# First row block of the scores from a joint key matmul, and three smaller moves, in a one-core encoder block

## The chip, the cores and the metric

The kernel runs on one core of one Trainium2 chip. The metric is the device time of one execution in microseconds, as the median of several; lower is better. A profiled execution gives, beside its time, a record of every instruction on the engines: PE (matmuls) and PEld (the weight loads that go with them), DVE (vector), ACT (scalar), POOL (a slower vector engine) and SP (here a queue that issues transfers).

## The reference

One layer of an encoder block on a 512 x 2048 input in float32, with eight stick-breaking heads (`sb`), eight forgetting heads (`fox`) and a squared-ReLU layer of width 8192. What matters here are the scores of a head, q k^T, block of 128 rows by block, each row block i with (i+1)*128 key columns:

```python
for i in range(seq // Q_BLOCK):
    end = (i + 1) * Q_BLOCK
    qb = q[:, :, i * Q_BLOCK:end]
    kb = k[:, :, :end]
    z = jnp.einsum('bhqd,bhkd->bhqk', qb, kb).astype(jnp.float32) * scale
    ...
x = x + jnp.einsum('bse,ed->bsd', mixed, w_out[l])
```

The fox heads add a bias to z and take a softmax; the sb heads take log-sigmoids, a reversed running sum and an exponential. Both end in a product with v, a per-head norm, and a slice of `mixed`, which the output projection multiplies.

## The kernel before

All matrix products run in a rounded 32-bit format. To keep float32 accuracy each operand is split in a high part (ACT casts it) and a low part (DVE subtracts: source minus high), and each product is three matmuls, high x high, high x low, low x high. `mm3` (lines 76 to 79) issues them, which is why most matmuls of the profile stand on L77, L78 and L79.

The stages in order: first projections (to about 160 us), the heads (about 165 to 610 us), the output projection (to about 750 us), and the two large layers to the end. The heads run as a pipeline of 17 periods of about 26 us, the eight fox heads first. In period n PE projects q and k of head n (`accq`, 96 matmuls), computes the scores of head n-1 into the PSUM tile `s` (`Head.scores`, L792), the product with v of head n-2 (tile `o`), and the two matmuls that sum squares for that head's norm (tile `ssq`, `norm_sums`, L938 and L939). A head's work between scores and product: fox adds the bias on DVE (`start`, L840), takes row maxima (L847), exponentials on ACT (L852), a scaling on DVE (L857); sb does absolute value, exponential and logarithm on ACT (L806 to L810), DVE and POOL work, and a last exponential (L823). The result `w` is transposed by a transfer, or for the last head on PE (`turn`, L867), and split (`ph`, `pl`, L884 and L887). After the product, `square` (L928 to L930) and `square_low` (L933) make the operands of `ssq`.

The order of the work in this stage is written out by hand: `plan.at(time, function)` puts each step at a planned time, `Plan.run` sorts by it, and for PE, ACT and DVE the program keeps that order. Each engine works through its own list in order; an instruction that waits holds everything behind it. The planned times only sort. SP's order is made by the scheduler after the first periods.

Between the heads' work the same stage prepares sums of the output weights, in pairs of blocks. `whole(m, t)` does the first four of these: `load` (two transfers of 1 MB, L968), then for each of two sides a cast and a subtraction (`high` L972, `low` L975, tile `tboth`, which is then stored), and four differences (`sum`, L980). For m = 1 the first side was planned at 10.7 and 11.15 us, and the first difference at 16.3 us, into a period.

The projections' weights come in pieces (`wraw`, L163), split by ACT (L170, tile `wh`) and DVE (L177, tile `wl`).

After the heads, `g_form` (through `a_form` and `split`, L59 and L60) makes seven split left operands `g` from `mixed`, piece by piece; `out_piece` multiplies them with the output weights into `accoa`, `accob` and `accoc`.

Of the kernel before, what the change touches and what calls it, by code (L numbers as in the profile page):

```python
# [8 lines left out]
F32 = mybir.dt.float32  # L9
F32R = mybir.dt.float32r  # L10
U16 = mybir.dt.uint16
AF = mybir.ActivationFunctionType
ALU = mybir.AluOpType
PSUM = bass.MemoryType.PSUM

P = 128
NT = 512
# [3 lines left out]
NH = 8  # L21
# [11 lines left out]
OFF_Q = [256, 0, 384, 768]  # L33
# [4 lines left out]
def block_kernel(ctx, tc, x, g_attn, w_in, b_f, g_out_sb, g_out_fox, w_out, g_mlp, w_up, w_down, g_final, y):  # L38
# [59 lines left out]
    def u_tile(c):  # L98
        return tuple(up.tile([P, NT], F32R, tag=f"u{p}{c}", name=f"u{p}") for p in "hl")
# [119 lines left out]
    with ExitStack() as stage:  # L219
# [23 lines left out]
        plan = Plan()  # L243
# [469 lines left out]
    with tc.tile_pool(name="att", bufs=1, side="right", reuse_waits="tile") as at, \  # L713
# [25 lines left out]
                dve.scalar_tensor_tensor(f, ps, SCALE, rb, op0=ALU.mult, op1=ALU.mult)  # L739

        def high_u(i, which):
            u_of[i, which] = u_tile(i % 2 * 2 + which)
            act.copy(u_of[i, which][0], now["qf"])

        def low_u(i, which):
# [27 lines left out]
        def rows(w):  # L773
            return [w[:, OFF_Q[i]:OFF_Q[i] + (i + 1) * P] for i in range(TB)]
# [12 lines left out]
        class Head:  # L787
# [4 lines left out]
            def scores(self):  # L792
                q, k = u_of[self.i, 0], u_of[self.i, 1]
                s = atp.tile([P, 1536], F32, tag="s", name="s")
                for i in (3, 2, 0, 1):
                    n = (i + 1) * P
                    qs = slice(i * P, (i + 1) * P)
                    mm3(s[:, 2 * P + OFF_Q[i]:2 * P + OFF_Q[i] + n], q[0][:, qs], q[1][:, qs], k[0][:, :n], k[1][:, :n], i != 0, True)
                self.s = s[:, 2 * P:]

            def plan_sb(self, plan, t):
                g = self.h
# [27 lines left out]
            def plan_fox(self, plan, t):  # L830
                h = self.h - NH

                def load():
                    self.cb = at.tile([P, NT], F32, tag="ul5", name="cb")
                    sp.dma_start(self.cb, ckd[h:h + 1, :].to_broadcast([P, NT]))

                def start():
                    w = self.w = wide("w")
                    for i, r in enumerate(rows(self.s)):
                        dve.scalar_tensor_tensor(rows(w)[i], r, cq[:, i, h:h + 1], self.cb[:, :(i + 1) * P], op0=ALU.add, op1=ALU.add)  # L840
                    causal(w, ALU.is_ge, NEG)

                def maxed():
                    ml = at.tile([P, P], F32, tag="ml", name="ml")
                    self.mx, self.l = ml[:, :TB], ml[:, 16:16 + TB]
                    for i, r in enumerate(rows(self.w)):
                        dve.tensor_reduce(self.mx[:, i:i + 1], r, axis=mybir.AxisListType.X, op=ALU.max)  # L847
                    dve.tensor_scalar(self.mx, self.mx, -1.0, None, op0=ALU.mult)

                def soft():  # L850
                    for i, r in enumerate(rows(self.w)):
                        act.activation(r, r, AF.Exp, bias=self.mx[:, i:i + 1], accum_out=self.l[:, i:i + 1])  # L852

                def scale():
                    dve.reciprocal(self.l, self.l)
                    for i, r in enumerate(rows(self.w)):
                        dve.tensor_scalar(r, r, self.l[:, i:i + 1], None, op0=ALU.mult)  # L857

                for dt, f in zip((-4.0, 7.5, 12.4, 14.8, 17.5), (load, start, maxed, soft, scale)):
                    plan.at(t + dt, f)  # L860
# [134 lines left out]
        def whole(m, t):  # L995
            w = WeightSums(m, (0, 1), lambda: mixed[:, :NH].rearrange("p (q a) n -> p q (a n)", a=2))
            e, o = (t, t + TPER) if m else (TPER, TPER)
            loads = (0.5 if m == 1 else -15.0, 2.7) if m else (20.5, 20.6)
            highs, lows_, sums_, sixth = ((e + 3.3, o + 3.3), (e + 4.5, o + 4.5), (e + 6.4, e + 16.3, o + 6.4, o + 16.3), (o + 10.7, o + 20.6)) if m > 1 else \
                ((e + 10.7, o + 3.3), (e + 11.15, o + 4.5), (e + 16.3, e + 24.9, o + 6.4, o + 16.3), (o + 10.7, o + 20.6)) if m else \  # L1000
                ((e + 4.0, e + 10.0), (e + 5.2, e + 11.0), (e + 6.4, e + 19.2, e + 20.6, e + 21.8), (e + 22.0, e + 24.0))
            for i in range(2):
                plan.at(t + loads[i], w.load, (i,))
                plan.at(highs[i], w.high, i)
                plan.at(lows_[i], w.low, i)
            for i in range(4):
                plan.at(sums_[i], w.sum, i)
            plan.at(sums_[1] + 0.1, lambda: w.store(0, 2))
            plan.at(sixth[0], w.high_6)
            plan.at(sixth[1], w.low_6)  # L1010
            plan.at(sixth[1] + 0.1, lambda: w.store(2, 4))
# [44 lines left out]
        for n in range(2 * NH + 1):  # L1056
# [49 lines left out]
            if 0 <= i_s < 2 * NH:  # L1106
                H = heads[i_s]
                plan.at(t + (5.45 if n < 2 * NH else 4.4), H.scores)
                sb = H.h < NH
                (H.plan_sb if sb else H.plan_fox)(plan, t)  # L1110
                if n < 2 * NH:
                    plan.at(t + (24.7 if sb else 22.0), H.halves)
                    plan.at(t + (24.8 if sb else 22.1), H.turn_halves)
                else:
                    tp = t + 1.45 * 14 + 1.95 - 0.05
                    plan.at(tp, H.turn)
                    plan.at(tp + 1.2, H.p_high)
                    plan.at(tp + 2.5, H.p_low)
                if i_s % 2 == 0 and i_s < 2 * NH - 2:
                    p_ = i_s // 2  # L1120
                    plan.at(t - (7.0 if sb else 12.0) if p_ else t + 3.0, load_v, p_)
                    plan.at(t + (4.3 if sb else 11.3 if p_ else 12.0), high_v, p_)
                    plan.at(t + (5.7 if sb else 24.9 if p_ else 16.35), low_v, p_)
# [345 lines left out]
    for db in range(2):  # L1469
        if db == 1:  # L1470
            begin(0, 0, db)
        else:

            for p in (1, 2):
                g_form(p, (4, 8), (0, 2), (2, 3))
            with tc.issue_after(last_heads[2].ins):
                for p in (4, 5):
                    g_form(p, (4, 8), (0, 2), (2, 3))
            more_parts.append(lambda: parts_at(px, "px"))
            out_piece(1, 0, 4)  # L1480
            with tc.issue_after(last_heads[3].ins):
                out_piece(1, 0, 6)
            with tc.issue_after(last_heads[2].ins):
                with tc.issue_after(last_heads[0].ins):
                    out_piece(1, 0, 0)
                    out_piece(2, 0, 4)
                with tc.issue_after(last_heads[1].ins):
                    out_piece(2, 0, 6)
                    out_piece(2, 0, 0)
            begin(0, 0, db)  # L1490
            for p in (1, 2, 4, 5):
                g_form(p, (3, 4))
            g_form(6, (4, 8), (0, 2), (2, 4))
            last_heads[4] = lows[0]
        for i, p in enumerate(G_ORDER):
            for m0 in (2,) if db == 0 and p in (1, 2) else (4, 6, 0, 2):
# [618 lines left out]
```

## Time and profile before

| | us |
|---|---|
| median of 3 runs | 2012.35 |
| lowest and highest of them | 2009.54 and 2012.75 |
| the profiled execution's own time | 2012.1 |
| its span, first to last instruction | 2010.4 |
| PE busy in the span | 1997.9 |
| DVE busy | 1738.8 |
| ACT busy | 1202.2 |
| POOL busy | 58.3 |

The span is 1.7 us shorter than the execution's time. In the rows of the profile a time is counted from the span's start, the second number is how long the instruction or the group took, and a bracket at the end of a row tells how long the engine sat idle before it and who released it. The rows on the waits give, for an engine and a line, the sum of its waits for another, how often, and the longest. [...]

### The profile page before, as it was taken

Reading aid. Unit: us, or ns where it says so; the run is one execution under the profiler, and the core shown is the slowest. Engines: PE = TensorE matmul, PEld = TensorE weight load, DVE = VectorE, ACT = ScalarE, POOL = GpSimd, SP = SyncE. Lnnn points to the kernel's source line nnn. Section 1 sums busy time; section 2 is a strip of 40 time slices with the busy share of each in tenths; the row PEclk is TensorE's granted clock in tenths of the full one; section 3 lists DMA queues with packets and bytes.
Section 4 is the critical chain, followed back from the end, with each engine's and each line's share of the span. In section 5 each row is a group of like instructions: output and inputs, shape, how many; then the busy total and the mean of one; then the engine's idle time right before and its main releaser. Section 6 shows DMA issues by size and latency. Waiting matters only on the chain.

```text
span 2010.4 us, 27058 instructions
## 1 busy us (share of the span) xinstructions
PE 1997.9 (99%) x10302; PEld 1730.5 (86%) x10302; DVE 1738.8 (86%) x1968; ACT 1202.2 (60%) x1645; POOL 58.3 (3%) x73
## 2 busy tenths in 40 slices
PE   9999999999999999999999999999999999999998
PEld 9998788888898889888888888888888888888887
DVE  7886777788878578999999999998798888988896
ACT  7544666777765565777676766767543444444344
POOL 0000000011110000000000000000000000000003
PEclk9999999999999999999999999999999999999999
DMA  7417877777668872566666676666794674674642
GB/s 253 161 68 247 269 241 215 212 212 217 207 218 279 292 255 95 172 208 209 207 190 211 194 222 189 210 199 235 252 327 172 232 273 153 234 264 170 216 161 86
DMA packets 309426, 423.54 MB, mean 211 GB/s; under 512 B 49408, under 2 KB 205104, under 8 KB 302768
## 3 DMA queue, kind: packets, MB, share of 16 engines
q1 hardware_dynamic: 308544, 419.71, 63.8%
q10 hardware_dynamic: 752, 2.11, 0.3%
q8 instruction: 81, 1.33, 0.3%
q14 instruction: 49, 0.40, 0.1%
HBM read 315.45 MB, written 96.49 MB: 205 GB/s over the span
## 4 chain that ended last, share of the span: by engine, by line
PE 96%; DVE 1%; DMA 1%; ACT 0%; SPq 0%; issue 0%; ACTq 0%; DVEq 0%
PE psa L1287 11%; PE accd L78 8%; PE accd L79 8%; PE accd L77 8%; PE psa L1285 6%; PE psc L1287 5%; PE accq L77 5%; PE accq L79 5%; PE accq L78 5%; PE psc L1285 3%; PE psb L1287 3%; PE psb L1285 1%; PE m L78 1%; PE m L77 1%; PE m L79 1%; PE accoa L79 1%
## 5 line engine op out<-in xcount | busy, mean ns | idle before, releaser
L1923 ACT CAST wh<-wd 128x1024 fp32r<-128x1024 f32 x126 | 124.9, 999 | 168.7 <-PE accd L79 61.0
L1809 DVE TENSOR_TENSOR wl<-wu,wh 128x1024 fp32r<-128x1024 f32 x158 | 192.8, 1220 | 12.1 <-ACT wh L1803 11.9
L77 PE MATMUL accq<-hH,wh 128*128 128x512 f32 x512 | 200.8, 392 | 0.0
L79 PE MATMUL accq<-hH,wl 128*128 128x512 f32 x512 | 200.1, 391 | 0.0
L78 PE MATMUL accq<-hL,wh 128*128 128x512 f32 x512 | 199.8, 390 | 0.0
L1803 ACT CAST wh<-wu 128x1024 fp32r<-128x1024 f32 x158 | 167.5, 1060 | 43.8 <-issue 26.7
L1287 PE MATMUL psa<-f,wh 128*128 128x512 f32 x720 | 179.0, 391 | 0.0
L78 PE MATMUL accd<-wl,uf 128*128 128x512 f32 x436 | 169.6, 389 | 0.0
L79 PE MATMUL accd<-wh,uf 128*128 128x512 f32 x436 | 169.6, 389 | 0.0
L77 PE MATMUL accd<-wh,uf 128*128 128x512 f32 x436 | 169.4, 389 | 0.0
L1287 PEld LDWEIGHTS psa<-f,wh 128*128 128x128 f32 x720 | 132.3, 188 | 25.6
L1930 DVE TENSOR_TENSOR wl<-wd,wh 128x1024 fp32r<-128x1024 f32 x126 | 144.1, 1152 | 10.6 <-ACT wh L1923 10.6
L1923 ACT CAST wx<-wd 128x1024 fp32r<-128x1024 f32 (+1 forms) x82 | 80.8, 994 | 106.9 <-PE accd L79 43.4
L1644 DVE TENSOR_TENSOR m<-m,accd 128x1024 f32<-128x1024 f32 x84 | 102.3, 1218 | 47.1 <-PE accd L79 47.1
L79 PEld LDWEIGHTS accq<-hH,wl 128*128 128x128 f32 x512 | 96.4, 188 | 20.4
L78 PEld LDWEIGHTS accq<-hL,wh 128*128 128x128 f32 x512 | 96.6, 189 | 19.3
L77 PEld LDWEIGHTS accq<-hH,wh 128*128 128x128 f32 x512 | 96.6, 189 | 19.0
L77 PE MATMUL accd<-wx,uf 128*128 128x512 f32 x284 | 110.5, 389 | 0.0
L78 PE MATMUL accd<-wx,uf 128*128 128x512 f32 x284 | 110.5, 389 | 0.0
L79 PE MATMUL accd<-wx,uf 128*128 128x512 f32 x284 | 110.5, 389 | 0.0
L1285 PEld LDWEIGHTS psa<-f,wl 128*128 128x128 f32 x720 | 96.0, 191 | 5.4
L1285 PE MATMUL psa<-f,wl 128*128 128x256 f32 x720 | 98.3, 282 | 0.0
(443 smaller groups left out, 5118.1 us busy)
## 6 DMA issues: line engine op xcount, KB each, us to landing
wu<-in_w_up_dram SPq DMA_DIRECT2D x60, 1024.0 KB, 6.5
ufd<-st SPq DMA_DIRECT2D x98, 512.0 KB, 3.9
wd<-in_w_down_dram SPq DMA_DIRECT2D x48, 1024.0 KB, 8.5
uf<-ufd SPq DMA_DIRECT2D x42, 1024.0 KB, 7.5
wraw<-in_w_in_dram SPq DMA_DIRECT2D x68, 512.0 KB, 6.0
wo<-wsums SPq DMA_DIRECT2D x28, 512.0 KB, 4.4
q<-in_w_in_dram SPq DMA_DIRECT2D x32, 384.0 KB, 5.6
wd<-in_w_down_dram SPq DMA_DIRECT2D x16, 768.0 KB, 5.4
```

The lines of the kernel that those rows point to most:

```text
L77: pe.matmul(out, sh, mh, start=first, stop=False, skip_group_check=True)
L78: pe.matmul(out, sh, ml, start=False, stop=False, skip_group_check=True)
L79: return pe.matmul(out, sl, mh, start=False, stop=last, skip_group_check=True)
L1285: ins = pe.matmul(ps[:, 2 * P:], lo[:, a, :], f_parts(p, a)[0], start=False, stop=last, skip_group_check=True)
L1287: ins = pe.matmul(ps, hi[:, a, :], f_both(p, a), start=a == PAIRS[0] and p in (1, 5), stop=last, skip_group_check=True)
L1644: dve.tensor_tensor(M[p][:, :, db, :], M[p][:, :, db, :], ps, op=ALU.add)
L1803: act.copy(rooms[k][0], srcs[k])
L1809: lows[0] = dve.tensor_tensor(lo, srcs.pop(k), hi.bitcast(F32), op=ALU.subtract)
L1923: act.copy(rooms[k + 3][0], srcs[k + 3])
L1930: dve.tensor_tensor(rooms[k + 2][1], srcs.pop(k + 2), rooms[k + 2][0].bitcast(F32), op=ALU.subtract)
```

## The change

Four edits. First, k of each head goes in one tile `uk` with the high and the low part side by side, and the first row block of the scores takes two matmuls where it took three: one with 256 columns (q high with k high and k low, which land in two neighbouring 128-column halves) and one with 128 columns (q low with k high, added into the left half). The halves must then be added. In a fox head DVE does it after the bias, with one more 128 x 128 operation; in an sb head by the new `first_row`, a copy of the right half and an addition into the place where the first row block stood. Second, the first side of the weight pair m = 1 is planned later in its period. Third, the left form 6 is made in smaller first steps. Fourth, `first_row` has a place of its own in the plan, for the last head an earlier one.

```diff
         def high_u(i, which):
-            u_of[i, which] = u_tile(i % 2 * 2 + which)
+            c = i % 2 * 2 + which
+            if which:
+                now["k", i] = up.tile([P, 2, NT], F32R, tag=f"u{c}", name="uk")
+                u_of[i, which] = now["k", i][:, 0], now["k", i][:, 1]
+            else:
+                u_of[i, which] = u_tile(c)
             act.copy(u_of[i, which][0], now["qf"])
...
-                for i in (3, 2, 0, 1):
+                for i in (3, 2):
...
-                    mm3(s[:, 2 * P + OFF_Q[i]:2 * P + OFF_Q[i] + n], q[0][:, qs], q[1][:, qs], k[0][:, :n], k[1][:, :n], i != 0, True)
-                self.s = s[:, 2 * P:]
+                    mm3(s[:, 2 * P + OFF_Q[i]:2 * P + OFF_Q[i] + n], q[0][:, qs], q[1][:, qs], k[0][:, :n], k[1][:, :n], True, True)
+                pe.matmul(s[:, :2 * P].rearrange("p (a n) -> p a n", a=2), q[0][:, :P], now.pop(("k", self.i))[:, :, :P], start=True, stop=False,
+                          skip_group_check=True)
+                pe.matmul(s[:, :P], q[1][:, :P], k[0][:, :P], start=False, stop=False, skip_group_check=True)
+                mm3(s[:, 2 * P:4 * P], q[0][:, P:2 * P], q[1][:, P:2 * P], k[0][:, :2 * P], k[1][:, :2 * P], False, True)
+                self.s, self.first = s[:, 2 * P:], s[:, :2 * P]
+
+            def first_row(self):
+                row = at.tile([P, P], F32, tag="row", name="row")
+                dve.tensor_copy(row, self.first[:, P:])
+                dve.tensor_tensor(self.s[:, 2 * P:3 * P], self.first[:, :P], row, op=ALU.add)
...
-                        dve.scalar_tensor_tensor(rows(w)[i], r, cq[:, i, h:h + 1], self.cb[:, :(i + 1) * P], op0=ALU.add, op1=ALU.add)
+                        s = self.first[:, :P] if i == 0 else r
+                        dve.scalar_tensor_tensor(rows(w)[i], s, cq[:, i, h:h + 1], self.cb[:, :(i + 1) * P], op0=ALU.add, op1=ALU.add)
+                    dve.tensor_tensor(rows(w)[0], rows(w)[0], self.first[:, P:], op=ALU.add)
                     causal(w, ALU.is_ge, NEG)
...
-                ((e + 10.7, o + 3.3), (e + 11.15, o + 4.5), (e + 16.3, e + 24.9, o + 6.4, o + 16.3), (o + 10.7, o + 20.6)) if m else \
+                ((e + 19.0, o + 3.3), (e + 20.55, o + 4.5), (e + 20.6, e + 24.9, o + 6.4, o + 16.3), (o + 10.7, o + 20.6)) if m else \
...
+                if sb:
+                    plan.at(t + (6.35 if n == 2 * NH else 8.2), H.first_row)
...
-            g_form(6, (4, 8), (0, 2), (2, 4))
+            g_form(6, (4, 6), (6, 8), (0, 2), (2, 4))
```

What the plan makes of it, at three places. The first is ACT in period 2, from the cast of the third weight piece of a projection to the first step of the norm (`tboth` is the weight pair's first side, `ph<-o` to `pl<-ph` the squares for `ssq`). Before:

```order
L170 CAST wh<-wraw 128x1024
L972 CAST tboth<-mixed 128x512
L170 CAST wh<-wraw 128x1024
L852 ACTIVATE w,ml<-w,ml 128x128
...
L852 ACTIVATE w,ml<-w,ml 128x512
L928 ACTIVATE ph<-o 128x512
L929 COPY os<-o 128x512
L930 CAST pl<-ph 128x512
L743 CAST uh<-qf 128x512
L942 ACTIVATE ra<-ssq,eps 128x512
```

Now:

```order
L170 CAST wh<-wraw 128x1024 x2
L868 ACTIVATE w,ml<-w,ml 128x128
...
L868 ACTIVATE w,ml<-w,ml 128x512
L944 ACTIVATE ph<-o 128x512
L945 COPY os<-o 128x512
L946 CAST pl<-ph 128x512
L748 CAST uh<-qf 128x512
L988 CAST tboth<-mixed 128x512
L958 ACTIVATE ra<-ssq,eps 128x512
```

The cast of the pair stood ahead of the fourth weight piece's cast and of the exponentials, and stands behind the squares. On DVE its subtraction and first difference move likewise, from ahead of the maxima and of the scaling to behind `pl<-ph,pl` (L933) and the low part of q.

The second is DVE in period 10, an sb head (`ws` is a later weight pair, `pl<-pt,ph` the low part for the product with v), from v's low part on. Before:

```order
L771 TENSOR_TENSOR vl<-vr,vh 128x1024
L980 TENSOR_TENSOR ws<-ws 128x512 x2
L887 TENSOR_TENSOR pl<-pt,ph 128x1280
```

Now:

```order
L776 TENSOR_TENSOR vl<-vr,vh 128x1024
L812 COPY row<-s 128x128
L813 TENSOR_TENSOR s<-s,row 128x128
L996 TENSOR_TENSOR ws<-ws 128x512 x2
L903 TENSOR_TENSOR pl<-pt,ph 128x1280
```

The two operations of `first_row` stand ahead of the weight pair's differences and of `pl`.

The third is DVE at the start of the output projection, from the first sum into the residual to the second (`g_5568` is the low part of form 6). Before:

```order
L1427 TENSOR_TENSOR x_5727<-x_5727,accoa 128x1024
L1207 TENSOR_TENSOR mixed<-mixed 128x256
L60 TENSOR_TENSOR g_5568<-mixed,g_5567 128x1024
L60 TENSOR_TENSOR g_5568<-mixed,g_5567 128x512
L1427 TENSOR_TENSOR x_5727<-x_5727,accob 128x1024
```

Now:

```order
L1445 TENSOR_TENSOR x_5727<-x_5727,accoa 128x1024
L60 TENSOR_TENSOR g_5568<-mixed,g_5567 128x512
L1225 TENSOR_TENSOR mixed<-mixed 128x256
L60 TENSOR_TENSOR g_5568<-mixed,g_5567 128x512 x2
L1445 TENSOR_TENSOR x_5727<-x_5727,accob 128x1024
```

The first piece of form 6 is half as long and stands one instruction earlier.

## The prediction

> **What bounds the kernel now.** I read the page first, then PE's waits, then the stretches around them.
>
> ```profile
> span 2010.4 us, 27058 instructions
> PE 1997.9 (99%) x10302; PEld 1730.5 (86%) x10302; DVE 1738.8 (86%) x1968; ACT 1202.2 (60%) x1645; POOL 58.3 (3%) x73
> PE 96%; DVE 1%; DMA 1%; ACT 0%; SPq 0%; issue 0%; ACTq 0%; DVEq 0%
> ...
> PE ssq L938 <- ACT pl L930: 2.5, 1, 2.5
> PE ssq L939 <- DVE pl L933: 0.5, 1, 0.5
> PE accoa L79 <- DVE g L60: 0.3, 1, 0.3
> ```
>
> PE is busy for 99% of the span and makes 96% of the chain of waits. So time comes off in two ways only: PE does less, or one of its few waits goes. The three rows of its waits are all there are between the first microseconds and the end (DVE and ACT being 86% and 60% busy costs nothing by itself). Two of them belong to one place, the squares' sum of the first head, and its price is more than its 3.0 us. The next rows are PE's matmuls around it, and the table of stretches that shows the granted clock.
>
> ```profile
> 220.75 0.39 PE L79 MATMUL accq<-hH,wl 128*128 128x512 f32 x1
> 223.59 0.50 PE L938 MATMUL ssq<-pl,onesr 128*128 128x512 f32 x1 [2.45 <-ACT pl L930]
> 224.59 0.78 PE L939 MATMUL ssq<-pl,onesr 128*128 128x512 f32 x1 [0.50 <-DVE pl L933]
> ...
> 228.12 0.40 PE L78 MATMUL accq<-hL,wh 128*128 128x512 f32 x1
> ...
> 221.20:224.60 3.40, 0.51 (x2) 0.20 (x2) 3.37 (x9) 2.85 (x8) 0.00 (x0) 1.00 0.89 302
> 224.60:228.05 3.45, 3.45 (x8) 2.77 (x9) 1.76 (x3) 2.60 (x3) 0.00 (x0) 0.51 0.00 1
> 228.05:231.50 3.45, 3.45 (x16) 2.81 (x16) 2.74 (x4) 0.93 (x1) 0.00 (x0) 1.00 0.46 104
> ```
>
> At full clock PE starts 16 matmuls in 3.45 us (the last row, twice the 8 of the row above it), and its 512-column matmuls follow each other every 0.227 us. From 220.75 to 228.12 stand ten steps (two `ssq`, eight `accq`); they should take 2.27 us and took 7.37. The place costs **5.1 us**: 3.0 of waiting, the rest the 3.45 us at a clock of 0.51 that followed a stretch in which PE ran two matmuls.
>
> Who is late there? ACT, then DVE:
>
> ```profile
> 206.40 8.94 DMA mixed<-in_w_out_dram
> ...
> 215.42 0.62 ACT L972 CAST tboth<-mixed 128x512 fp32r<-128x512 f32 x1 [3.42 <-DMA mixed<-in_w_out_dram]
> 216.94 1.05 ACT L170 CAST wh<-wraw 128x1024 fp32r<-128x1024 f32 x1 [0.90 <-DMA wraw<-in_w_in_dram]
> 219.77 0.40 ACT L852 ACTIVATE w<-w,ml 128x128 f32<-128x128 f32 x1 [1.78 <-DVE ml L848]
> 222.91 0.62 ACT L930 CAST pl<-ph 128x512 fp32r<-128x512 f32 x1
> ...
> 216.07 0.69 DVE L975 TENSOR_TENSOR tboth<-mixed,tboth 128x512 fp32r<-128x512 f32 x1 [3.49 <-ACT tboth L972]
> 220.19 1.21 DVE L177 TENSOR_TENSOR wl<-wraw,wh 128x1024 fp32r<-128x1024 f32 x1
> 223.85 0.69 DVE L933 TENSOR_TENSOR pl<-ph,pl 128x512 fp32r<-128x512 f32 x1
> ```
>
> The output weights for m = 1 land 8.94 us after their issue. ACT stands 3.42 us for them, DVE 3.49 us behind ACT, and the maxima, exponentials and squares are queued after both.
>
> **The pair moved later.** Now ACT goes from the third weight piece straight to the fourth. But that piece has its own transfer, and it lands at 216.94: the 0.90 us in that row. Nothing ahead of it on SP is moved, so I let it land at the same time; one wait takes over most of the other's place. The maxima no longer matter: DVE, without its 3.49 us, has them done before. From there by the rows: the cast ends its turn at about 217.9; from the first exponential to the end of the squares' cast took 222.91 + 0.62 - 219.77 = 3.76 us, so the cast ends at 221.66 and PE's first `ssq` can start at 221.72, by the 0.06 us between the two rows before. PE is ready at 220.98, less what two heads' scores have saved by then (0.23, below), 220.75. It waits 0.97. The low part on DVE follows the cast; from its start to PE's second `ssq` were 0.74 us (223.85 to 224.59), so that one starts at 222.44, a second wait of 0.49. Together 1.46 us of idling in place of 3.0, and PE busy for over half of any 3.4 us there, so I take the clock to stay. The eighth `accq` then starts at 222.44 + 8 x 0.227 = 224.25 where it started at 228.12: **3.87 us**. Bounds: 1.7 less if the clock falls all the same (half of 3.45), 1.2 more if the piece lands in time. The 0.69 and 1.22 us of `tboth` and the first difference go behind `ssq` on DVE, ahead of the norm and then of the next k; their cover is the slack of k's low part, next head's rows:
>
> ```profile
> 232.21 0.69 DVE L737 TENSOR_TENSOR qf<-accq,rb 128x512 f32<-128x512 f32 x1 [1.35 <-PE accq L79]
> 233.59 0.69 DVE L747 TENSOR_TENSOR ul<-qf,uh 128x512 fp32r<-128x512 f32 x1 [0.69 <-ACT uh L743]
> ...
> 237.61 0.23 PE s L77
> ```
>
> The low part of k ends at 234.28, 3.33 us ahead of the scores, and DVE idled 1.35 us ahead of k.
>
> **The scores.** One head's first row block and second, then the next projection:
>
> ```profile
> 183.73 0.23 PE L77 MATMUL s<-uh 128*128 128x128 f32 x1
> ...
> 184.01 0.34 PE L77 MATMUL s<-uh 128*128 128x256 f32 x1
> ...
> 184.43 0.39 PE L77 MATMUL accq<-hH,wh 128*128 128x512 f32 x1
> ```
>
> Six matmuls, three of 128 and three of 256 columns, take 0.70 us: 0.117 each whatever their width. If columns set the pace, 128 of them would cost a quarter of 0.227, 0.057, and the first three 0.17 and not the 0.28 that they take. So here the number of matmuls counts, each with its weight load, and one fewer saves 0.115 us a head. Bounds: nothing, if only columns counted (384 before and after), and 0.17 if the new five ran by columns from the start of the block. I take 0.115: the six even steps are the nearest row. Two of the heads are in the place above; the other 14 give **1.6 us**. [...]
>
> **The additions on DVE.** The trace has no 128-column addition out of PSUM; the nearest rows bound it:
>
> ```profile
> L840 DVE SCALAR_TENSOR_TENSOR w<-s,cq,cb 128x128 f32<-128x128 f32 x8 | 2.8, 351 | 8.3 <-PE s L79 7.0 <-DMA cb<-ckd 1.4
> L857 DVE TENSOR_SCALAR w<-w,ml 128x128 f32<-128x128 f32 x8 | 2.3, 287 | 0.3
> ...
> 448.69 0.69 DVE L980 TENSOR_TENSOR ws<-ws 128x512 f32<-128x512 f32 x1 [1.46 <-DMA ws<-in_w_out_dram]
> 449.96 0.69 DVE L980 TENSOR_TENSOR ws<-ws 128x512 f32<-128x512 f32 x1 [0.57 <-DMA ws<-in_w_out_dram]
> 450.57 1.48 DVE L887 TENSOR_TENSOR pl<-pt,ph 128x1280 fp32r<-128x1280 f32 x1
> 453.68 0.28 PE L78 MATMUL o<-pl,vh 128*128 128x256 f32 x1
> ```
>
> Between 0.29 and 0.35 us each; I take 0.33, so 0.33 in a fox head and about 0.7 for the pair in an sb head. An sb head has room: the pair falls where DVE waits 1.46 and 0.57 us for a transfer, and `pl`, ending at 452.05, is 1.63 us ahead of the matmul that reads it. Without that cover it would still cost nothing up to 1.63. The last head is tighter, because ACT starts on its scores at once and PE waits for what comes of it:
>
> ```profile
> 577.71 1.24 ACT L806 ACTIVATE w<-s 128x1280 f32<-128x1280 f32 x1 [3.04 <-PE s L79]
> 593.65 1.52 POOL L779 TENSOR_SCALAR_AFFINE_SELECT w<-w 128x256 f32<-128x256 f32 x2 [6.78 <-ACT w L823]
> 596.04 1.25 PE L867 MATMUL pt<-ident,w 128*128 128x128 f32 x10
> ```
>
> POOL is done at 595.17, 0.87 us ahead of the transposes. The pair eats 0.7 and one cast that now stands ahead of the exponential some 0.1. I cost it at nothing; if it is 0.3 longer than I think, 0.3 us.
>
> **Form 6 in smaller steps.**
>
> ```profile
> 624.10 0.39 PE L78 MATMUL accoa<-wx,g 128*128 128x512 f32 x1
> 624.77 0.50 PE L79 MATMUL accoa<-wx,g 128*128 128x512 f32 x1 [0.29 <-DVE g L60]
> 625.12 0.40 PE L77 MATMUL accoa<-wx,g 128*128 128x512 f32 x1
> ...
> 623.50 1.82 DVE L60 TENSOR_TENSOR g<-mixed,g 128x1024 fp32r<-128x1024 f32 x2
> ```
>
> From 624.10 to 625.12 two steps take 1.02 us where 0.45 was due: 0.57 lost. The first piece is now 512 wide and starts one instruction (0.33) earlier: ready at about 623.85, ahead of 624.33. I take **0.5**, between 0 and 0.57.
>
> **Sum.** 3.87 + 1.6 + 0.5 = 6.0 us off the profiled execution's 2012.1 (span 2010.4 and 1.7 around it): 2006.1. The median of the runs shown is 0.25 higher, so I say **2006.2**.
>
> **Rivals.** (a) The clock falls all the same, because 1.46 us of idling is enough: 1.7 us back, 2007.9. For it: between the 0.29 us that left the clock alone and the 3.0 that did not, the trace shows nothing. 0.13. [...] (b) The columns set the scores' price: no saving there, 2007.8. Against it the even steps. 0.07. (c) The fourth piece lands earlier, as ACT and DVE let it go: no wait, 2005.0. 0.08. (d) The change does not do what it says at the first head: the piece lands 1.5 us later with the traffic around it, and wait and slow clock stay: 2012.3 - 1.6 - 0.5 = 2010.2. 0.08. (e) Slower: the moved pair stalls the next head. DVE's `tboth` stands ahead of the norm, the last difference and the next k. If it waits for its staging buffer's store or its data, k's low part is late; room is the 3.3 us and the 1.35 of idling, less 1.9 of moved work, about 2.8. To end slower than before it must be late by some 9 us (6.0 us of gain and 2.8 of room; from some 7 on if the clock falls with it). Against it: the data landed at 215.34, 7 us before. 0.14, mostly for what I do not see. My forecast keeps 0.50.
>
> **How the numbers follow.** Under 0.2%, 4.0 us, a measurement of this kernel cannot be told from no change; that line is at 2008.3. The forecast, (a), (b) and (c) lie below it, 0.78, of which I move 0.08 to "same" for a sum a little too good: faster 0.70, same 0.16 with (d), slower 0.14. The range takes in the bounds of every term and (d) in part: 2003.9 to 2010.0; what is left out is (e) and half of (d), 0.18.
>
> **What would show it.** PE's waits for `ssq` of 1.0 and 0.5 us in place of 2.5 and 0.5, the first with ACT waiting about 4.9 us for `wraw` ahead of it; a clock of 1.00 in the stretch after; five score matmuls in 0.58 us; no wait of `accoa` at form 6; `first_row` at 0.7 us with no new wait of PE. A new PE wait in a period after the second, or at the last head's transposes, would prove the sum wrong, as would the wait for `ssq` unchanged.

## The result, and the profile after

The changed kernel's median is 2005.91 us of 8 runs (2004.14 to 2006.74), that of the kernel before, measured beside it, 2012.07 us of 8 (2009.54 to 2012.99). The ratio is 0.9971, with an interval of 0.9962 to 0.9979: 4.2 to 7.6 us less. The profiled execution took 2004.53 us, with a span of 2002.8.

The page of the changed kernel, and all the waits of PE (us in total, times, the longest):

```profile
span 2002.8 us, 27063 instructions
PE 1993.1 (100%) x10286; PEld 1726.8 (86%) x10286; DVE 1746.4 (87%) x1994; ACT 1201.8 (60%) x1646; POOL 67.0 (3%) x73
...
PE vx L303 <- DVE still L299: 1.6, 1, 1.6
PE ssq L955 <- DVE pl L949: 0.2, 1, 0.2
```

The first wait stands in the first microseconds of both kernels. Of the 3.0 us at the first head's `ssq` 0.2 is left in this view (and a first `ssq` 0.1 us late, too little to be listed), and the wait at form 6 is gone. The place itself, on PE, ACT and DVE, and the two stretches of granted clock around it:

```profile
219.47 0.39 PE L79 MATMUL accq<-hH,wl 128*128 128x512 f32 x1
219.79 0.50 PE L954 MATMUL ssq<-pl,onesr 128*128 128x512 f32 x1
220.52 0.50 PE L955 MATMUL ssq<-pl,onesr 128*128 128x512 f32 x1 [0.23 <-DVE pl L949]
...
222.45 0.39 PE L78 MATMUL accq<-hL,wh 128*128 128x512 f32 x1
...
215.03 1.05 ACT L170 CAST wh<-wraw 128x1024 fp32r<-128x1024 f32 x1 [4.88 <-DMA wraw<-in_w_in_dram]
215.98 0.40 ACT L868 ACTIVATE w<-w,ml 128x128 f32<-128x128 f32 x1
...
213.82 0.17 DVE L864 TENSOR_SCALAR ml<-ml 128x4 f32<-128x4 f32 x1
...
216.96:220.37 3.41, 3.33 (x14) 2.25 (x12) 2.41 (x7) 3.41 (x10) 0.00 (x0) 1.00 1.01 372
220.37:223.78 3.41, 3.26 (x14) 2.74 (x15) 3.34 (x6) 3.10 (x4) 0.00 (x0) 1.00 0.46 170
```

The ten steps from 219.47 to 222.45 take 2.98 us, where they took 7.37 and 2.27 are due. They are timed from start to start, as matmul rows overlap: in the kernel before, those of 512 columns are 0.39 us long and start 0.227 us apart. ACT now stands 4.88 us for the weight piece instead of 3.42 for the pair and 0.90 for the piece, but it goes on at 215.03 and not at 216.94. Of these 1.91 us, 1.28 are only PE's earlier place in this execution (next table). The larger part is behind it: the maxima are done (213.82 + 0.17), so the exponentials follow at once, at 215.98, where they waited another 1.78 us for the maxima before. The clock stays at 1.00 (the number behind the five engines).

One head's first two row blocks, the start of form 6, and the cover of `first_row` in period 10 and in the last head:

```profile
182.65 0.29 PE L804 MATMUL s<-uk,uh 128*128 128x256 f32 x1
182.78 0.22 PE L806 MATMUL s<-uk,ul 128*128 128x128 f32 x1
...
183.25 0.40 PE L77 MATMUL accq<-hH,wh 128*128 128x512 f32 x1
...
616.97 0.39 PE L78 MATMUL accoa<-wx,g 128*128 128x512 f32 x1
617.20 0.39 PE L79 MATMUL accoa<-wx,g 128*128 128x512 f32 x1
...
441.69 0.29 DVE L812 COPY row<-s 128x128 f32<-128x128 f32 x1 [0.88 <-PE s L79]
442.01 0.30 DVE L813 TENSOR_TENSOR s<-s,row 128x128 f32<-128x128 f32 x1
...
444.35 0.69 DVE L996 TENSOR_TENSOR ws<-ws 128x512 f32<-128x512 f32 x1 [1.45 <-DMA ws<-in_w_out_dram]
444.96 1.49 DVE L903 TENSOR_TENSOR pl<-pt,ph 128x1280 fp32r<-128x1280 f32 x1
447.07 0.28 PE L78 MATMUL o<-pl,vh 128*128 128x256 f32 x1
...
586.86 1.52 POOL L784 TENSOR_SCALAR_AFFINE_SELECT w<-w 128x256 f32<-128x256 f32 x2 [6.78 <-ACT w L837]
588.92 1.25 PE L883 MATMUL pt<-ident,w 128*128 128x128 f32 x10
```

The five matmuls take 0.60 us (182.65 to 183.25), the six took 0.70. Form 6 starts without a gap. The product's low part in period 10 ends 0.62 us ahead of the matmul that reads it (446.45 to 447.07), where it had 1.63; POOL in the last head is 0.54 us ahead of PE, where it was 0.87. Cover was eaten, nothing came through.

Where the 7.6 us between the two spans came from is read by the start of the same matmul in both traces:

| matmul | before | changed | lead | gained since the row above |
|---|---|---|---|---|
| the first `accq`, ahead of all heads | 63.19 | 62.11 | 1.08 | 1.08 |
| the last `accq` ahead of the first head's `ssq` | 220.75 | 219.47 | 1.28 | 0.20 |
| the eighth `accq` behind it | 228.12 | 222.45 | 5.67 | 4.39 |
| the fourth `accoa` | 593.99 | 586.86 | 7.13 | 1.46 |
| end of the span | 2010.4 | 2002.8 | 7.6 | 0.5 |

The lead of the first row is there at 12 us already, where nothing was changed; the 0.20 of the second are the scores of the first two heads. This is the stretch from 5 to 10 us of the kernel before, and then of the changed one:

```profile
5.00:10.00 5.00, 5.00 (x25) 4.79 (x24) 2.64 (x6) 2.37 (x4) 0.00 (x0) 1.00 0.95 316
```

```profile
5.00:10.00 5.00, 4.79 (x34) 4.07 (x34) 3.11 (x7) 2.67 (x5) 0.00 (x0) 1.00 0.96 304
```

PE starts 25 matmuls in it before and 34 after. The record of the granted clock begins, at full speed, at 9.60 us in the one execution and at 5.33 in the other (the column's 1.00 ahead of that stands for no record); in the other profiles below it begins between 5.06 and 9.41. Two of these, the changed kernel again and the last version with the pair back, are the same program as the changed kernel in their first microseconds and begin it at 5.83 and 9.41; so it goes with the execution and not with the change, and it is part of the spread of the runs.

### The profile page after: what moved, and what is told of

It is laid out like the page before. It is cut to its first block, busy times and chain, and to the rows that moved or that the text cites. A ratio compares the mean times of both kernels' runs of the same rounds, so it can differ in the third digit from the quotient of the medians.

```text
span 2002.8 us, 27063 instructions
## 1 busy us (share of the span) xinstructions
PE 1993.1 (100%) x10286; PEld 1726.8 (86%) x10286; DVE 1746.4 (87%) x1994; ACT 1201.8 (60%) x1646; POOL 67.0 (3%) x73
## 4 chain that ended last, share of the span: by engine, by line
PE 97%; DMA 1%; DVE 1%; ACT 0%; issue 0%; SPq 0%; ACTq 0%; DVEq 0%
PE psa L1305 11%; PE accd L78 8%; PE accd L77 8%; PE accd L79 8%; PE psa L1303 6%; PE psc L1305 5%; PE accq L77 5%; PE accq L79 5%; PE accq L78 5%; PE psc L1303 3%; PE psb L1305 3%; PE psb L1303 1%; PE m L77 1%; PE m L78 1%; PE m L79 1%; PE accoa L77 1%
```

## The experiments

Each kernel ran on one chip beside the kernel before, and its ratio is to that. "Ten steps" are always the two `ssq` of the first head and the eight `accq` around them, 2.27 us when nothing waits.

### The pair alone, and all but the pair

```diff
-                ((e + 10.7, o + 3.3), (e + 11.15, o + 4.5), (e + 16.3, e + 24.9, o + 6.4, o + 16.3), (o + 10.7, o + 20.6)) if m else \
+                ((e + 19.0, o + 3.3), (e + 20.55, o + 4.5), (e + 20.6, e + 24.9, o + 6.4, o + 16.3), (o + 10.7, o + 20.6)) if m else \
```

This line alone, in the kernel before:

> The kernel before with one edit of the four: the first side of the weight pair m = 1 later. Theory A (each edit acts at its own place and the places add): PE's ten steps around the first head's ssq, 7.4 us before, take 3.0 to 3.5; the clock stays at 1.00 behind them; the wait of accoa at form 6 (0.29 us) stays, and the six score matmuls of a head's first two row blocks still take 0.70 us. Time 4.4 us under before, ratio 0.9978. Rival B (the wait went because the edits together put PE and ACT elsewhere in time, the pair alone does little): the wait of 2.5 us or the slow clock stays, at most 2.5 us come off, ratio above 0.9988.

Measured: 2007.67 us, ratio 0.9981 (0.9972 to 0.9990). The waits of PE:

```profile
PE ssq L938 <- ACT pl L930: 0.9, 1, 0.9
PE accoa L79 <- DVE g L60: 0.3, 1, 0.3
PE ssq L939 <- DVE pl L933: 0.2, 1, 0.2
```

The ten steps take 3.97 us, a gain of 3.40, though 3.0 to 3.5 us were expected; the clock stays, form 6 still waits. The weight piece's cast started at 216.12 here, 3.50 us ahead of PE's last `accq` (219.62); in the changed kernel's profile it was 4.44 us ahead (215.03 and 219.47). The piece's landing floats against PE from execution to execution. Five of the profiles below (the changed kernel again, and the runs on idling, on widths, on `first_row` and on the moved pair) have the changed kernel's order up to this place: there the cast was 2.97 to 3.93 us ahead, and the ten steps took 3.54 to 4.10 us in four of them and 6.04 in the fifth, where the clock fell. So the changed kernel's first profile, with 2.98, is the luckiest of six.

One of the ten executions of this kernel took 2012.39 us, with a mean granted clock of 0.997 where the others have 0.999 and 2007.33 to 2008.58 us. Its clock fell somewhere; no trace of it tells where.

The same line taken out of the changed kernel:

> The changed kernel with the first side of the weight pair m = 1 put back where it was; scores, first row and form 6 as changed. Theory A (places add): the ten steps around the first head's ssq take about 7.4 us again with ssq waiting 2.5 and 0.5 us and one stretch of 3.4 us at a clock of 0.5; 1.4 to 1.6 us come off in 14 heads and 0.5 at form 6; time 2.0 us under before, ratio 0.9990. Rival B: the first head's wait is shorter than 2 us without the pair's move, because PE and DVE stand elsewhere; ratio 0.998 or less.

Measured: 2010.64 us, ratio 0.9993 (0.9984 to 1.0002), which alone tells little: 1.4 us under the kernel before, where 2.0 were expected. The trace tells more. The waits of PE, and the stretches of granted clock:

```profile
PE ssq L954 <- ACT pl L946: 2.6, 1, 2.6
...
218.81:222.22 3.41, 1.14 (x6) 0.60 (x4) 3.37 (x7) 3.41 (x11) 0.00 (x0) 1.00 1.00 392
222.22:225.64 3.42, 2.89 (x6) 1.99 (x7) 1.88 (x4) 2.01 (x5) 0.00 (x0) 0.50 0.39 119
225.64:229.05 3.41, 3.41 (x9) 2.64 (x9) 3.19 (x5) 2.31 (x2) 0.00 (x0) 0.50 0.00 0
```

The wait is back, and this time two stretches at half clock follow instead of one, 1.1 us more than in the kernel before. Behind it the heads bring 1.4 us and form 6 0.5, as in the changed kernel. So the places add, theory A; rival B falls in both runs.

### The same order without the transfer

In the kernel before, the first side of pair m = 1 reads another tile, `rb`, at its old place; this kernel leaves out that side of the pair, so its output is not the layer's:

```diff
-                act.copy(self.both[:, 0], self.q[(0, 2)[i]][:, :NT])
+                act.copy(self.both[:, 0], rb if self.m == 1 and i == 0 else self.q[(0, 2)[i]][:, :NT])
```

(and the subtraction likewise).

> The kernel before; the first side of the weight pair m = 1 stands at its old place on ACT and DVE, but both read rb, a tile that has long landed, in place of the weights, so that side of the pair is not computed. Theory A (ACT's wait for the weights' transfer, with DVE behind it, was the cause): ACT no longer waits 3.4 us there but some 4 to 5 us for the fourth weight piece, and the ten steps around ssq take 3.0 to 3.5 us at full clock. Rival C (the pair's work standing ahead of the maxima and exponentials was the cause: a 0.5 us cast on ACT, 0.6 and 1.1 us on DVE): ssq still waits 1.5 us or more for ACT, and the ten steps take 4.5 us or more.

Measured: 2007.68 us, one run. ACT around the cast, and PE's waits:

```profile
211.27 0.62 ACT L972 CAST tboth<-rb 128x512 fp32r<-128x512 f32 x1
216.29 1.05 ACT L170 CAST wh<-wraw 128x1024 fp32r<-128x1024 f32 x1 [4.41 <-DMA wraw<-in_w_in_dram]
...
PE ssq L938 <- ACT pl L930: 0.5, 1, 0.5
```

The ten steps take 3.52 us, at the edge of the 3.0 to 3.5 expected. The cast and the subtraction stand where they stood and cost next to nothing; their wait for data was the price. Rival C falls.

### The rest of the wait

First by PE: the two `ssq` six matmuls later.

```diff
+                if n == 2:
+                    marks[3:4] = [(3, 0, 2, 20.2), (3, 2, 4, 20.3)]
                 for a, k0, k1, dt in marks:
```

> The changed kernel with PE's two ssq matmuls of the first head six matmuls (1.36 us) later among the projection's, nothing else. Theory A (what is left of that wait, about 0.7 us in all, goes; the norm has room for 1.4 us): no PE wait between 10 us and the end over 0.2 us, ten steps around ssq in 2.3 us, time 0.7 us under the changed kernel, 6.9 us under before, ratio 0.9966. Rival D (the norm that follows, on ACT and DVE, then makes the next k late): a new wait of PE at the scores of the third head, time equal to the changed kernel's or above.

Measured: 2004.23 us of 5, ratio 0.9963 (0.9949 to 0.9976). The second `ssq` still waits 0.2 us in the view: the piece's cast began at 215.96, 0.9 us later than in the changed kernel's profile with PE 0.2 us earlier, and took most of the shift. No wait at the scores, so rival D falls. Of theory A's 0.7 us this execution shows 0.26 (2.72 us for the ten steps against 2.98); against the four profiles with 3.54 to 4.10 it is 0.8 to 1.4, as the wait there is not a constant.

Then by ACT, where the transfer no longer stands ahead of the exponentials (PE reads that piece in the next period):

```diff
+                        if a == 0 and n == 3:
+                            cast, low = -8.0, -6.4
```

> The changed kernel; the weight piece that ACT waits for in the first head's place (4.9 us there; PE reads it only in the next period) is cast behind the squares in place of ahead of the exponentials, and its subtraction on DVE behind the squares' low part. Theory A (the only thing that still delays ssq is that transfer): the exponentials start some 0.1 us after the maxima, no wait of ssq, ten steps around ssq in 2.3 us whenever the piece lands; PE 0.7 us less than in the changed kernel, time about 2005.2, ratio 0.9966. Rival D (the later subtraction frees the piece's buffer later, SP's next piece and what is queued behind it come late): a new wait of PE in the next two periods, time 2006 or more.

Measured: 2004.18 us of 6, ratio 0.9967 (0.9955 to 0.9980). ACT and PE at the place, and all waits of PE:

```profile
214.23 0.40 ACT L868 ACTIVATE w<-w,ml 128x128 f32<-128x128 f32 x1 [3.58 <-DVE ml L864]
217.37 0.62 ACT L946 CAST pl<-ph 128x512 fp32r<-128x512 f32 x1
...
219.55 0.39 PE L954 MATMUL ssq<-pl,onesr 128*128 128x512 f32 x1
...
PE vx L303 <- DVE still L299: 1.6, 1, 1.6
```

The squares' cast ends at 217.99, 1.56 us ahead of PE, and from the first microseconds on PE has no wait at all. Against the changed kernel once more, side by side:

> The changed kernel once more, beside the kernel with the piece cast behind (e10) in the same call. Theory A: as before, 2004 to 2007, ratio to the kernel before 0.9970; the wait at the first head's ssq is 0.1 to 1.1 us, by when the piece lands in this execution.

> The kernel of e10 once more. Theory A (no wait of ssq whatever the transfer does): again no wait at ssq, and a median 0.4 to 1.5 us under the changed kernel's of the same call. Rival D (e10's lower time was the spread of the executions): the two medians within 0.3 us or the other way round.

Measured: the changed kernel 2005.69 us of 5 (2004.66 to 2005.83), ratio 0.9968 (0.9956 to 0.9981), with its first `ssq` waiting 0.5 us and the ten steps 1.4 us over (3.63); the other 2004.08 us of 5 (2003.57 to 2005.16), ratio 0.9962 (0.9949 to 0.9976), no wait. The medians are 1.6 us apart, a little more than the 0.4 to 1.5 expected, and the intervals overlap; in both profiles of the other the wait is gone. Its medians, 2004.18 and 2004.08 us, are the lowest here; the later sums, with 2004.23, cannot be told from it.

Last, that version with the pair back at its old place:

> The kernel of e10 with the first side of the weight pair back where it was before the change, so that of the two transfers that ACT waited for ahead of the exponentials only the pair's is left there. Theory A (each of the two suffices to delay ssq; the pair's lands about 1.5 us ahead of the piece's, but DVE's subtraction, a weight piece's low part and the maxima are queued behind it): ssq waits 2.0 to 2.7 us for ACT, ten steps in 5 us or more, more if the clock falls. Rival K (the weight piece's wait did most of it, and the pair's move mattered little): ssq waits under 1 us.

Measured: 2009.50 us, one run. ACT and DVE:

```profile
214.94 0.62 ACT L988 CAST tboth<-mixed 128x512 fp32r<-128x512 f32 x1 [3.10 <-DMA mixed<-in_w_out_dram]
219.29 0.40 ACT L868 ACTIVATE w<-w,ml 128x128 f32<-128x128 f32 x1 [3.73 <-DVE ml L864]
...
215.59 0.69 DVE L991 TENSOR_TENSOR tboth<-mixed,tboth 128x512 fp32r<-128x512 f32 x1 [3.17 <-ACT tboth L988]
217.33 1.66 DVE L863 TENSOR_REDUCE ml<-w 128x1 f32<-128x128 f32 x4
```

`ssq` waits 2.3 us for ACT and one stretch at half clock follows: 5.0 us over the changed kernel's profile, 1.0 of it from the start. The pair's transfer does it by way of DVE: the maxima stand behind `tboth` there, and ACT's exponentials wait 3.73 us for them. Rival K falls.

### How much idling the clock takes

```diff
+        IDLE = (0, 6, 7, 8, 9, 10, 11, 10, 11, 12, 13, 14, 15, 16, 0, 0)
...
-                act.copy(self.os, self.o)
+                for _ in range(1 + IDLE[self.i]):
+                    act.copy(self.os, self.o)
```

> The changed kernel with a copy on ACT ahead of the squares' cast repeated, 6 to 11 more times in heads 1 to 6 and 10 to 16 in heads 7 to 13 (about 0.47 us each, slack 1.8 and 3.7 us), to make PE idle ahead of ssq by about 1.0 to 3.4 us and 1.0 to 3.8. The clock is granted in stretches of 3.41 us whose phase is fixed from the start. Theory E (the idle share of one such stretch decides: 1.5 us of 3.41 left the clock alone, 2.4 made it fall): the clock falls where a stretch holds 2.4 us of idling or more, also where PE ran a matmul in it; a wait of 2.5 us cut by the edge of a stretch does not. Rival F (only a stretch without any matmul): no fall below 3.4 us of unbroken waiting. Rival G (the length of the wait alone, wherever the edges are): one threshold between 1.3 and 2.6 us parts the heads.

Measured: 2091.45 us, one run; 14 waits of `ssq` for ACT, 55.2 us in all, up to 6.4 us each and so longer than the 3.8 planned. The place with the shortest wait that brought the clock down, head 1:

```profile
247.40:250.81 3.41, 1.75 (x6) 1.23 (x7) 1.90 (x3) 2.56 (x5) 0.00 (x0) 1.00 0.00 0
250.81:254.23 3.42, 3.42 (x10) 2.65 (x9) 2.65 (x4) 2.84 (x2) 0.00 (x0) 0.50 0.78 305
```

Idling is counted here between matmul starts: what a step takes beyond its due time (0.227 us at full clock for 512 columns, about 0.115 for 256, and by the author's estimate twice that at half; the product of the kernel before takes 0.118 each for six of 256, 453.56 to 454.27, and in its stretch at half clock those of 512 start 0.43 us apart). The stretches follow from the clock's own changes: in this run it changed at 5.06, 250.81, 254.23 and 281.54 us, which are 72, 1 and 8 times 3.413 us apart. In the heads (160 to 620 us) of all the profiles of this study together:

| stretch of 3.41 us | idle in it | how many | clock in the next |
|---|---|---|---|
| at full clock | 1.23 to 1.90 us | 6 | full |
| at full clock | 2.04 to 3.41 us | 18 | half |
| at half clock | 0 to 0.61 us | 18 | full |
| at half clock | 0.77 to 3.02 us | 7 | half |

Theory E holds in these profiles, with a threshold between 1.90 and 2.04 us, lower than its 2.4. Rival F falls: six matmuls in the stretch did not save the clock of head 1. Rival G falls by two runs below: a wait of 1.4 us, with 0.5 more lost behind it in the same stretch, brought the clock down, and one of 1.75 us did not. The table's lower half was not expected: the clock came back behind the 18 stretches at half clock with 0.61 us of idling or less and behind none of the 7 with 0.77 or more, one of which is the first of the two that the run with the pair put back paid for.

### Widths of the score matmuls

```diff
...
+                if self.i < NH:
+                    pe.matmul(s[:, :2 * P].rearrange("p (a n) -> p a n", a=2), q[1][:, :P], both[:, :, :P], start=False, stop=False,
+                              skip_group_check=True)
+                    mm3(s[:, 2 * P:4 * P], q[0][:, P:2 * P], q[1][:, P:2 * P], k[0][:, :2 * P], k[1][:, :2 * P], False, True)
+                else:
+                    pe.matmul(s[:, :P], q[1][:, :P], k[0][:, :P], start=False, stop=False, skip_group_check=True)
+                    for c in range(2):
+                        cs = slice(c * P, (c + 1) * P)
+                        mm3(s[:, (2 + c) * P:(3 + c) * P], q[0][:, P:2 * P], q[1][:, P:2 * P], k[0][:, cs], k[1][:, cs], False, True)
```

> The changed kernel with other widths in the first two row blocks: in fox heads the second matmul (q low) is 256 columns wide in place of 128, the count is the same; in sb heads the second row block is cut in six matmuls of 128 columns in place of three of 256, the columns are the same. Theory N (up to 256 columns a matmul costs 0.116 us, its weight load, whatever its width): fox heads' five matmuls take 0.58 us as in the changed kernel, sb heads' eight take 0.93, 0.35 more; 2.8 us more in eight sb heads. Rival C (columns: 0.057 us for 128): fox heads 0.06 more, sb heads as before.

Measured: 2007.76 us, one run. A fox head, then an sb head:

```profile
233.76 0.29 PE L805 MATMUL s<-uk,uh 128*128 128x256 f32 x1
...
234.36 0.40 PE L77 MATMUL accq<-hH,wh 128*128 128x512 f32 x1
...
442.33 0.29 PE L805 MATMUL s<-uk,uh 128*128 128x256 f32 x1
...
443.19 0.45 PE L77 MATMUL accq<-hH,wh 128*128 128x512 f32 x1
```

Fox: 0.60 us as in the changed kernel, though 128 columns were added. Sb: 0.86, 0.26 more for three more matmuls at the same columns. So the count sets the price, theory N, but at 0.107 us each (0.86/8) in place of 0.116. By the starts the eight sb heads lose 2.35 us against the changed kernel's profile, 0.29 each, of which 0.03 come in the first `accq` behind the block; 0.35 each and 2.8 in all were expected. The rows of the weight loads themselves show 0.19 us each and overlap; that it is the weight load which sets the price of a narrow matmul, as theory N has it, is not shown.

### How much `first_row` may cost, and the moved pair

```diff
-                dve.tensor_copy(row, self.first[:, P:])
+                for _ in range(13 if self.i < 2 * NH - 1 else 1):
+                    dve.tensor_copy(row, self.first[:, P:])
```

> The changed kernel; in the sb heads but the last, first_row's copy stands 13 times in place of once, 12 x 0.21 to 0.29 = 2.5 to 3.5 us more on DVE. Theory H (first_row is covered by DVE's wait for the weight pair and the slack of the product's low part): in the period where the product's low part had 0.62 us of slack and DVE waited 1.45 us for a transfer, 2.07 us are covered and PE waits 0.4 to 1.4 us at o; in the other six at most 1.7. Rival J (cover is much larger, DVE's idle time is far more than that): no new wait of PE.

Measured: 2021.79 us, one run; PE waits for `pl` at `o` in all seven heads, 11.0 us together. Two of the heads:

```profile
398.31 0.39 PE L78 MATMUL o<-pl,vh 128*128 128x256 f32 x1 [1.75 <-DVE pl L904]
...
447.45 4.19 DVE L813 COPY row<-s 128x128 f32<-128x128 f32 x13
...
454.74 0.58 PE L78 MATMUL o<-pl,vh 128*128 128x256 f32 x1 [2.52 <-DVE pl L904]
```

Thirteen copies took 4.19 us: each repeat cost 0.325 us, not 0.21 to 0.29, so 3.9 were added and not 2.5 to 3.5. PE waited 2.52 of them in the period for which 0.4 to 1.4 were expected; the cover there was 1.4 us, not 2.07. In the other six at most 1.7 us was expected, and 0.57 to 2.48 came. Rival J falls, theory H holds in kind and is too generous by 0.7 us.

```diff
-                dve.tensor_tensor(self.both[:, 1], self.q[(0, 2)[i]][:, :NT], self.both[:, 0].bitcast(F32), op=ALU.subtract)
+                for _ in range(9 if self.m == 1 and i == 0 else 1):
+                    dve.tensor_tensor(self.both[:, 1], self.q[(0, 2)[i]][:, :NT], self.both[:, 0].bitcast(F32), op=ALU.subtract)
```

> The changed kernel with the moved subtraction of the weight pair's first side done nine times on DVE in place of once, 8 x 0.72 = 5.8 us more ahead of the norm and the next head's k. Theory A (k's low part has 2.9 us of slack there and covers that much): PE waits about 2.9 us at the scores of the third head, and since that is more than the 2.0 us of idling in one stretch that made the clock fall, one or two stretches at 0.5 follow, 1.7 us or more; 4.6 to 6.5 us in all. Rival L (the pair's store, which SP issues behind the subtraction, holds SP's next transfers, the transposition of the head first of all): the first new wait of PE is at the product o in the period after, and the scores wait less than 2 us.

Measured: 2010.40 us, one run. All PE waits behind the start:

```profile
PE ssq L954 <- ACT pl L946: 1.4, 1, 1.4
PE ssq L955 <- DVE pl L949: 0.7, 2, 0.5
PE s L77 <- ACT uk L748: 0.5, 1, 0.5
PE o L78 <- DVE pl L903: 0.4, 1, 0.4
PE s L78 <- DVE uk L752: 0.2, 1, 0.2
```

The scores lost 1.2 us by the starts, not 2.9, and the clock did not fall there. The weight piece landed late in this execution: `ssq` waited 1.4 us ahead of the repeats and the clock fell, so that PE left the place 2.9 us behind the changed kernel's profile, while DVE began the repeats only 1.3 us behind it. 5.8 of repeats + 1.3 - 2.9 of PE's delay - 2.9 of slack = 1.3 us, near the 1.2 that came. The first new wait is at the scores, so rival L falls, and theory A's mechanism stands with this correction, which was made after the run.

## Why the prediction was right

**The bound.** Three waits, two places: right. Both places went. Behind the start the profile shows 0.20 + 4.39 + 1.46 + 0.5 = 6.55 us, where 6.0 were predicted, and the medians differ by 6.2. The profile's span shows 7.6, of which 1.1 is the start. The 6.55 of this one profile are partly luck, as the next term shows; the medians are the better comparison.

**The pair moved later**, 3.87 us predicted up to the eighth `accq`, two heads' scores included; 4.59 measured (5.67 less the 1.08 of the start). The step "I let it land at the same time" was right in the middle and not in each execution. Predicted were 1.46 us of idling. The ten steps were 0.71 us over in the changed kernel's first profile, 1.36 in its second, 1.70 with the pair alone, 1.27 to 1.83 in three more profiles with the same order, and 3.77 in a fourth, where the clock fell. So 1.46 is near the middle, and the 0.7 us by which this term was too small belong to one lucky execution. The bound for a piece that lands in time should have been 1.46 more, the whole idling, and not 1.2. ACT's wait of 4.9 us for `wraw`, its place ahead of the exponentials and the clock of 1.00 came as said. That one wait would take over from another was the right reading; that it belonged to a piece which PE reads a period later, and could be moved too, was not seen in the prediction.

**The scores**, 1.6 us predicted, 1.46 measured. The matmul that fell away was worth 0.100 us (0.695 to 0.595), not 0.115: the joint one takes 0.13 to the next start. The term was 0.2 us too large, the mechanism right: the number of matmuls set the price. But the six steps were not even, as the prediction has it: its own rows give 0.28 us for the three of 128 columns and 0.42 for the three of 256, so they spoke less clearly against columns than it says; that the count decides was settled by the run on widths only.

**The additions.** `first_row` takes 0.53 us (441.69 to 442.22) where 0.7 was predicted, and no wait came of it; but the "1.63 us" of cover in period 10 fell to 0.62. There DVE waits for `ws`, which came 2.72 us ahead of the matmul and not 3.72 as before: it was the transfer's place that took the 1.0 us, and why it moved was not followed. In the last head 0.87 fell to 0.54.

**Form 6**, 0.5 predicted, 0.5 measured.

**The rivals.** (a), the clock at 1.46 us of idling: the threshold is at 1.9 to 2.0, so the forecast was on the right side by some 0.4 us, which the trace of before could not show. It can come true in single executions: in the run with the subtraction repeated, whose order up to there is the changed kernel's, 2.06 us of idling brought the clock down. The two profiles of the changed kernel itself do not show it, and none of its 13 executions took more than 2006.74 us. (b) falls by the widths. (c), no wait at all, needed one more move. (d) and (e) did not come; with 5.8 us of extra work ahead of k one run was still 1.6 us under the median of the kernel before, so (e) was far off.

## What to carry to other kernels

Where one engine is busy for 99%, its few waits are the list of what can be had; price each by the starts of the instructions around it, clock and all, and then ask what the engine behind the wait would wait for next. An operand that comes by a transfer should stand in an in-order engine's list behind everything that doesn't need it: moving one such cast brought 3.4 us, moving the next the 0.7 to 1.4 that were left. A narrow matmul is worth joining with a neighbour only while its price does not depend on its width: here up to 256 columns (0.595 us for the five matmuls, 0.602 with 128 columns more), and no longer at 384 (0.17 to 0.18 us each).

## What the runs showed of the hardware

The granted clock of PE changed at steps of 3.413 us from where its record begins in the execution: 63 and 1 of them in the kernel before (9.60, 224.63 and 228.05 us), 72, 1 and 8 in the run on idling. In the heads of the profiles here all 18 stretches at full clock with 2.04 us of idling or more were followed by one at half clock, 14 of them with matmuls in them, head 1's with six; the 6 with 1.23 to 1.90 us were not, and all 7 at half clock with 0.77 us of idling or more were followed by another. The price of a wait thus depended on where it lay in a stretch: with the pair back the same kind of wait cost 6.2 us and not 5.1.

The start of the record at full clock moved by up to 4.5 us between executions (5.06 to 9.60 us; in the kernel before, matmuls of 264 columns start 0.22 us apart ahead of its 9.60 and 0.12 behind it), and PE's first `accq` by up to 1.8 (61.42 to 63.19), so two single executions should be compared from a matmul behind the start and not by their spans.

A product of two 128x512 tiles took POOL 1.29 us in the kernel before (`m<-m,gf`, L1997, median of 14) and DVE 0.69 (`last<-m,gf`, L1995).
